# Dense products in portions of three beside a recurrence, and an earlier load of its first chunk's operands

## The chip, the cores and the metric

The kernel runs on one core of a Trainium2 chip. The metric is the time of one execution on the device, in microseconds (us). A core has a matrix engine (TensorE, in the profile PE, with its weight loads as PEld), a vector engine (VectorE, DVE), a scalar engine (ScalarE, ACT), GpSimd (POOL) and a queue engine (SyncE, SP). Each takes its own instructions strictly in order and waits on semaphores for the others; DMAs are issued from the queues of SP and ACT.

## The reference

Two residual layers over 512 positions and 1024 channels: a gated spatial MLP with its feed-forward part, then an RWKV-7 time mixer with its feed-forward part, then a last norm. The change lies in the time mixer. Cut to that:

```python
r, k, v = xr @ w_r, xk @ w_k, xv @ w_v
w = -softplus(-(w0 + tanh(xw @ w1) @ w2)) - 0.5
a = sigmoid(a0 + (xa @ a1) @ a2)
g = sigmoid(xg @ g1) @ g2
...
def step(state, inp):                       # 512 steps, 16 heads, state 64x64
    r_t, w_t, k_t, v_t, a_t, b_t = inp
    sa = einsum('bhvk,bhk->bhv', state, a_t)
    state = state * w_t + sa[..., None] * b_t + v_t[..., None] * k_t
    return state, einsum('bhvk,bhk->bhv', state, r_t)
...
y = group_norm(y) * ln_w + ln_b + bonus
return (y * g) @ w_o
```

## The kernel before

Everything is kept transposed: a tile is 128 channels by 512 positions, and there are eight of them (`KT`). A dense product is done in three matmuls of 128x512 (`mm3`, L291 to L297): the weight and the operand are each split into a high and a low part, and three of the four products are summed. The text counts such single matmuls as **dense products**; `mm3` issues three.

The recurrence is cut into eight **chunks** of 64 positions, and the sixteen heads into eight **pairs** (two heads fill 128 partitions). Within a chunk the recurrence is a small triangular system, so that the work has these stages, all in `rwkv_main`:

1. `pairs()` (L909) prepares for each pair the operands of all chunks: decays, keys, products between positions. They go to DRAM (`std`, `btd`, `vtd`) by SP's DMAs (L861, L895, L906, L790).
2. `invert(g)` (L936) inverts the 64x64 triangular blocks of four pairs: a loop of 31 steps with two DVE instructions each (L964, L965), two DVE transposes (L970, L971), copies by ACT (L975, L993, L995) and small matmuls (L985, L988).
3. `scan(g)` (L1079) walks through the eight chunks for four pairs, first `g` = 0, then `g` = 1. One chunk is a chain: L1105 and L1109 (PE, with the state) give `us` and `e`; DVE copies `us` to `wt` (L1107); L1118 applies the inverse; DVE and ACT copy the two halves to `vu` (L1119, L1120); L1125 gives the new state, which DVE adds into the next chunk's `vu` (L1128); L1130 gives the output, copied by ACT (L1133). The text calls the chunks **A0 to A7** (`scan(0)`) and **B0 to B7** (`scan(1)`). After every second chunk `finish` (L1141) normalizes the output (L1146 to L1159, with four PE transposes, L1156).
4. `load(g, c)` (L1061) brings a chunk's operands from DRAM: `st` in two DMAs of 384 KB together, `vu` in two, `cbt` in one, into rings of three tiles (`SCAN`).

Three generators hold the dense work: `projections()` (L733, the k and v products; with each v tile also `value`, L778: four matmuls L784 that count as eight instructions, one product with `wb`, L798, then DVE L800 and ACT L801), `gates()` (L998: per channel tile an operand made by ACT L1010, DVE L1011, ACT L213 and DVE L214, then six products into two accumulators) and `project()` (L1174, the output products with `w_o`).

What sets the order: `weave` (L1254) runs a main generator and after each of its yields adds `rate` portions from `fill` (a portion is what `fill` does up to its next yield) and half a step of a side generator (`invert`). A portion of `dense_steps` (L196) holds `ktiles` calls of `mm3`: with `STEPS` all 2, six products. The framework's scheduler then sets each engine's final order by its own estimates, so the written order is not the executed one. Before, `fill` holds `projections()` alone up to the end of `scan(0)`; what is left is drained, and only for `scan(1)` does `fill` become `gates()` and `project()`. `load(0, 0)` stands after the pool of the pairs is closed (L1223), in the pool that takes its place.

## Time and profile before

| | us |
|---|---|
| median of 3 runs | 1329.78 (1329.23 to 1330.55) |
| the profiled execution | 1334.18 |
| its span | 1332.4 |
| from the last dense product ahead of A0 to the end of that stretch's dense work | 752.9 to 957.8 |

A page of the profile gives busy time per engine, a view by windows gives it for stretches of time with the granted clock of PE (PEclk, 1.00 is full speed), and the timeline gives single instructions: start, duration, engine, line, operation, output and inputs, shape, count, and in brackets how long the engine had been idle and what released it. A PE duration is longer than the distance to the next start, since matmuls are pipelined; the distance between starts is what a matmul costs. A small fp32 matmul is two PE instructions.

The scans' chunks start, by their first L1105 (A0 by the end of the dense work ahead of it), at 752.9 (A0), 770.3 (A1), 779.2, 789.7, 800.3 (A4), 808.3, 816.5, 831.0 (A7), 836.1 (B0), 840.4 (B1), 858.3 (B2), 867.4, 875.1, 885.2, 900.7 (B6) and 908.8 (B7). The first instruction behind the stretch, L330, starts at 957.8.

### The profile page before, as it was taken

How to read it: one execution, taken by the hardware profiler on the slowest of the kernel's cores; microseconds unless marked ns; L12 is line 12 of the kernel's file. 1: busy time of each engine (PE TensorE's matmuls, PEld its weight loads, DVE VectorE, ACT ScalarE, POOL GpSimd, SP SyncE). 2: the span in 40 equal slices, each digit the busy share in tenths (PEclk: the TensorE clock that was granted, in tenths of full speed). 3: DMA queues.
4: the chain of work that ended last, by engine and by line, in shares of the span. 5: the costliest groups of instructions: out<-in, count | busy, mean ns of one | idle time of the engine just before them, and what ended most of it. 6: DMA issues, size and time to landing. Idle time of an engine off the chain costs nothing.

```text
span 1332.4 us, 19460 instructions
## 1 busy us (share of the span) xinstructions
PE 1277.4 (96%) x7578; PEld 1025.6 (77%) x7578; DVE 853.5 (64%) x1371; ACT 630.7 (47%) x1072; POOL 142.1 (11%) x148
## 2 busy tenths in 40 slices
PE   8999999999999999999999797799999999999996
PEld 6778888888888888677777666567888888888886
DVE  5565487887884444857788573576677777773223
ACT  5444365555553333656775443343554445452221
POOL 3100200000000001211210112123300000000001
PEclk9999999999999999999999887899999999999998
DMA  7232355555566653247778765683233333332322
GB/s 260 83 111 79 111 160 171 167 166 166 168 187 223 214 180 107 80 140 213 204 216 247 189 156 119 140 211 98 79 95 95 95 96 99 102 95 87 103 87 75
DMA packets 101100, 189.06 MB, mean 142 GB/s; under 512 B 16976, under 2 KB 48464, under 8 KB 101008
## 3 DMA queue, kind: packets, MB, share of 16 engines
q10 hardware_dynamic: 36592, 109.46, 27.1%
q1 hardware_dynamic: 64416, 78.36, 20.8%
q8 instruction: 59, 0.97, 0.3%
q14 instruction: 33, 0.27, 0.1%
HBM read 146.63 MB, written 41.16 MB: 141 GB/s over the span
## 4 chain that ended last, share of the span: by engine, by line
PE 76%; DVE 8%; DMA 4%; issue 3%; ACT 3%; POOL 1%; ACTq 0%; SPq 0%; DVEq 0%; POOLq 0%
PE mm L295 8%; PE mm L296 7%; PE mm L297 7%; PE aux L296 5%; PE aux L295 5%; PE aux L297 5%; PE us L295 5%; PE us L297 5%; PE us L296 5%; PE e L297 5%; PE e L296 5%; PE e L295 5%; DVE tt L965 1%; DVE pr L964 1%; PE e L1130 1%
## 5 line engine op out<-in xcount | busy, mean ns | idle before, releaser
L213 ACT CAST wh<-w 128x512 fp32r<-128x512 f32 x356 | 217.0, 612 | 386.4 <-PE mm L296 105.7
L214 DVE TENSOR_TENSOR wl<-w,wh 128x512 fp32r<-128x512 f32 x348 | 240.9, 693 | 180.0 <-ACT wh L213 178.6
L295 PE MATMUL mm<-mxh,wh 128*128 128x512 f32 (+1 forms) x384 | 157.4, 410 | 1.6 <-DVE h L1196 1.2
L297 PE MATMUL mm<-mxh,wl 128*128 128x512 f32 (+1 forms) x384 | 153.1, 399 | 0.4 <-DVE wl L214 0.3
L296 PE MATMUL mm<-mxl,wh 128*128 128x512 f32 (+1 forms) x384 | 152.2, 396 | 0.0
L322 POOL TENSOR_TENSOR ss<-ss,sq 128x512 f32<-128x512 f32 x30 | 41.9, 1397 | 776.5 <-issue 594.8
L518 ACT ACTIVATE cv<-z,par 128x512 f32<-128x512 f32 x88 | 71.7, 817 | 36.0 <-DVE z L516 35.9
L295 PEld LDWEIGHTS mm<-mxh,wh 128*128 128x128 f32 (+1 forms) x384 | 72.2, 188 | 20.6 <-issue 3.6
L297 PEld LDWEIGHTS mm<-mxh,wl 128*128 128x128 f32 (+1 forms) x384 | 72.3, 189 | 18.2 <-issue 0.9
L295 PE MATMUL e<-mxh,wh 128*128 128x512 f32 x216 | 84.5, 391 | 0.0
L296 PEld LDWEIGHTS mm<-mxl,wh 128*128 128x128 f32 (+1 forms) x384 | 72.6, 189 | 14.9 <-issue 0.7
L296 PE MATMUL e<-mxl,wh 128*128 128x512 f32 x216 | 84.1, 389 | 0.0
L297 PE MATMUL e<-mxh,wl 128*128 128x512 f32 x216 | 84.0, 389 | 0.0
L296 PE MATMUL aux<-mxl,wh 128*128 128x512 f32 x208 | 81.4, 391 | 2.7 <-POOL mxl L214 2.0
L295 PE MATMUL aux<-mxh,wh 128*128 128x512 f32 x208 | 81.5, 392 | 0.3 <-ACT mxh L213 0.3
L519 DVE SCALAR_TENSOR_TENSOR cv<-z,par,cv 128x512 f32<-128x512 f32 x88 | 66.1, 752 | 23.9 <-ACT cv L518 23.9
L295 PE MATMUL us<-mxh,wh 128*128 128x512 f32 x208 | 81.3, 391 | 0.0
L297 PE MATMUL aux<-mxh,wl 128*128 128x512 f32 x208 | 81.0, 389 | 0.0
L297 PE MATMUL us<-mxh,wl 128*128 128x512 f32 x208 | 81.0, 389 | 0.0
L296 PE MATMUL us<-mxl,wh 128*128 128x512 f32 x208 | 80.9, 389 | 0.0
L520 DVE SCALAR_TENSOR_TENSOR cv<-z,par,cv 128x512 f32<-128x512 f32 x88 | 66.0, 752 | 2.9
L296 PEld LDWEIGHTS aux<-mxl,wh 128*128 128x128 f32 x208 | 39.1, 188 | 12.3 <-POOL mxl L214 2.7
(1074 smaller groups left out, 2715.8 us busy)
## 6 DMA issues: line engine op xcount, KB each, us to landing
w<-in_wup ACTq DMA_DIRECT2D x88, 512.0 KB, 3.6
w<-in_wdn ACTq DMA_DIRECT2D x32, 512.0 KB, 3.6
st<-std SPq DMA_DIRECT2D x32, 384.0 KB, 5.8
std<-lq SPq DMA_DIRECT2D x32, 256.0 KB, 4.4
w<-in_wdn ACTq DMA_DIRECT2D x16, 384.0 KB, 3.2
w<-in_wsu ACTq DMA_DIRECT2D x8, 512.0 KB, 3.7
w<-in_wso ACTq DMA_DIRECT2D x8, 512.0 KB, 3.6
pw<-in_wk SPq DMA_DIRECT2D x16, 256.0 KB, 3.4
```

What stands on the lines that cost most here:

```text
L213: nc.scalar.copy(hi[r, :n], src)
L214: (lo_eng or nc.vector).tensor_tensor(lo[r, :n], src, hi[r, :n].bitcast(F32), ALU.subtract)
L295: mm(acc, wh, xh, start=first, stop=False)
L296: mm(acc, wh, xl, start=False, stop=False)
L297: mm(acc, wl, xh, start=False, stop=last)
L322: nc.gpsimd.tensor_tensor(self.ss, self.ss, self.sq, ALU.add)
L518: nc.scalar.activation(c, z[:, 2:], AF.Identity, scale=cw(2, i), bias=self.p("conv_b", l * 44 + i))
L519: nc.vector.scalar_tensor_tensor(c, z[:, 1:T + 1], cw(1, i), c, ALU.mult, ALU.add)
L520: nc.vector.scalar_tensor_tensor(c, z[:, 0:T], cw(0, i), c, ALU.mult, ALU.add)
L964: V.tensor_tensor(q, a, b, ALU.mult)
L965: V.tensor_tensor(tt[:, 0:nj, j + 1:32], tt[:, 0:nj, j + 1:32], q, ALU.add)
L1130: nc.tensor.matmul(e[H[hd], 0, i, :], pt(i, hd), vu[H[hd], hd, i, :], start=False, stop=True, skip_group_check=True)
```

## The change

Three things change. `fill` is one chain of `projections()`, `gates()` and `project()` from the start, so that the gates' products can follow the projections within `scan(0)`. In both scans a portion holds one `mm3`, and the gates yield after each of their two accumulators, while the rates go from 0.65 to 1.15 and from 0.9 to 1.6 portions per yield. And `load(0, 0)` is called ahead of the last pair's stretch: its `st` goes as eight DMAs into four free tiles of the operand ring (`mxh`, `mxl`), its `cbt` and `vu` into the scratch tiles `ss` and `rb`; the ring of three then serves A1 onwards.

```diff
-RATES = ((1.9, 2), (1.9, 6, 2.2), (0.65, 2, 1), (0.9, 2), (2, 2), (0.7, 6, 2.2))
-LEAD = 3
+RATES = ((1.9, 2), (1.9, 6, 2.2), (1.15, 2, 1), (1.6, 2), (2, 2), (0.7, 6, 2.2))
+LEAD = 4
-FIRST0, WAIT, STEPS = 1, 1, (2, 2, 2, 2, 2)
+FIRST0, WAIT, STEPS = 1, 1, (2, 2, 1, 1, 2)
...
                     self.mm3(a, self.wcols(w, k * n, n), x, k == 0, k == KT - 1)
-                yield
+                    yield
...
             ps = slice(4 * g, 4 * g + 4)
-            st = tile_([P, 4 * 3 * P + P], "st", SCAN)
-            bt, vu = tile_([P, 4, 2, C], "cbt", SCAN), tile_([P, 2, 4, C], "vu", SCAN)
-            for hd in range(2):
-                o = P * (1 - hd)
-                nc.sync.dma_start(st[H[hd], o:o + 12 * P], std[g][c, H[hd]].rearrange("p i t -> p (i t)"))
+            if g == c == 0:
+                st = [t for _ in range(2) for t in (self.xr.tile([P, T], F32, tag=tag, bufs=10, name=self.uid(tag))
+                                                    for tag in ("mxh", "mxl"))]
+                bt = scratch("ss").rearrange("p (i a f) -> p i a f", i=4, a=2)
+                vu = scratch("rb").rearrange("p (a i f) -> p a i f", a=2, i=4)
+                for i in range(4):
+                    for hd in range(2):
+                        o = P * (1 - hd)
+                        nc.sync.dma_start(st[i][H[hd], o:o + 3 * P], std[g][c, H[hd], i])
+            else:
+                t = tile_([P, 4 * 3 * P + P], "st", SCAN)
+                st = [t[:, 3 * P * i:3 * P * i + T] for i in range(4)]
+                bt, vu = tile_([P, 4, 2, C], "cbt", SCAN), tile_([P, 2, 4, C], "vu", SCAN)
+                for hd in range(2):
+                    o = P * (1 - hd)
+                    nc.sync.dma_start(t[H[hd], o:o + 12 * P], std[g][c, H[hd]].rearrange("p i t -> p (i t)"))
...
-        fill = projections()
+        fill = itertools.chain(projections(), gates(), project())
+        gw = {}
...
+        load(0, 0)
         self.weave(main, inv, fill, *RATES[5], ktiles=STEPS[1])
...
-        gw = {}
-        load(0, 0)
...
-        for _ in fill:
-            pass
-        fill = itertools.chain(gates(), project())
```

From L1064 on the changed kernel's lines stand 12 lower in the scan (L1105 becomes L1117, L1118 L1130, L1125 L1137, L1130 L1142, L1156 L1168).

**Counts by the order.** On PE the order is the same up to the first L1105. From there to L330 both kernels hold 342 dense products; by chunk:

| chunks | before | now |
|---|---|---|
| A0 | 6 | 9 |
| A1, A2, A3 | 13, 16, 7 | 12, 9, 12 |
| A4, A5, A6, A7 | 0, 0, 0, 0 | 0, 6, 6, 12 |
| B0, B1 | 0, 14 | 12, 12 |
| B2 to B6 | 18, 10, 12, 42, 14 | 12, 21, 15, 30, 15 |
| B7 and behind it | 190 | 159 |

They stand in 57 unbroken runs before and in 72 now.

**First place: PE at the start of A0.** Before (`us`, `e` are the chunk's accumulators, `st`, `vu` its loaded operands, `mm` the dense accumulator, with `wh` its weight):

```order
L297 MATMUL mm_6774<-mxh_5578,wl_6645 128x512
L1105 MATMUL us_6731<-vu_6668,st_6666 64x64
L1109 MATMUL e_6732<-vu_6668,st_6666 64x64
L1105 MATMUL us_6731<-vu_6668,st_6666 64x64 x7
L1109 MATMUL e_6732<-vu_6668,st_6666 64x64 x7
L1118 MATMUL us_6731<-wt_6741,ti_4912 64x64 x8
L784 MATMUL mm_6849<-cst,v_6772 128x128 x3
L1130 MATMUL e_6732<-vu_6668,st_6666 64x64
L784 MATMUL mm_6849<-cst,v_6772 128x128
L1125 MATMUL us_6731<-vu_6668,cbt_6667 64x64 x8
```

Now, at the same place:

```order
L1121 MATMUL e_6758<-rb_6572,mxl_6570 64x64 x2
L784 MATMUL mm_6785<-cst,v_6731 128x128 x4
L295 MATMUL mm_6733<-mxh_5585,wh_6663 128x512
L296 MATMUL mm_6733<-mxl_5586,wh_6663 128x512
L297 MATMUL mm_6733<-mxh_5585,wl_6664 128x512
L1130 MATMUL us_6757<-wt_6767,ti_4912 64x64 x8
L295 MATMUL mm_6733<-mxh_5629,wh_6663 128x512
L798 MATMUL mm_6814<-rt_4387,wb_6812 128x512
L296 MATMUL mm_6733<-mxl_5630,wh_6663 128x512
L297 MATMUL mm_6733<-mxh_5629,wl_6664 128x512
L1137 MATMUL us_6757<-rb_6572,ss_6571 64x64 x8
```

The chunk reads `rb` and the ring tiles in place of `vu` and `st`, and dense work now stands on both sides of the inverse's product (`wt`), where before nothing stood ahead of it.

**Second place: DVE between A3 and A4**, where the inverse of the second four pairs ends (`tt`, `pr`, `ix`, `li` are its tiles). Before, the start of A3's copy `wt`, now that of A4's:

```order
L800 TENSOR_TENSOR rt_4387<-mm_7090,v_6979 128x512
L970 STREAM_TRANSPOSE ix_7268<-tt_6678 128x32x32
L971 STREAM_TRANSPOSE li_7269<-tt_6678 128x32x32
L1107 COPY wt_7031<-us_7021 128x256
L1159 SCALAR_TENSOR_TENSOR rt_4386<-aux_7044,par,rt_4386 128x128 x4
L1119 COPY vu_6917<-us_7021 64x256
```

```order
L965 TENSOR_TENSOR tt_6687<-tt_6687,pr_6688 128x31
L970 STREAM_TRANSPOSE ix_7302<-tt_6687 128x32x32
L1119 COPY wt_7155<-us_7145 128x256
L800 TENSOR_TENSOR rt_4387<-mm_7212,v_7197 128x512
L971 STREAM_TRANSPOSE li_7303<-tt_6687 128x32x32
L1131 COPY vu_7047<-us_7145 64x256
```

The two transposes have moved from A3 to A4, one ahead of the copy `wt`, the other between it and the copy `vu`.

**Third place: PE in A5** (`aux` is the accumulator of four transposes and of the inverse, `mm` now that of the gates). Before, then now:

```order
L1109 MATMUL e_7235<-vu_7126,st_7124 64x64 x7
L1156 MATMUL aux_7257<-cst,y_6923 128x128 x4
L1118 MATMUL us_7234<-wt_7244,ti_4912 64x64 x8
L985 MATMUL aux_7293<-ix_7268,ti_4913 32x32 x32
L1130 MATMUL e_7235<-vu_7126,st_7124 64x64
L1125 MATMUL us_7234<-vu_7126,cbt_7125 64x64 x8
```

```order
L1121 MATMUL e_7269<-vu_7138,st_7136 64x64 x7
L1168 MATMUL aux_7291<-cst,y_6938 128x128 x4
L296 MATMUL mm_7306<-mxl_7312,w_1392_7252 128x512
L297 MATMUL mm_7306<-mxh_7311,w_1393_7253 128x512
L1130 MATMUL us_7268<-wt_7278,ti_4912 64x64 x8
L985 MATMUL aux_7333<-ix_7302,ti_4913 32x32 x32
L295 MATMUL mm_7307<-mxh_7311,wh_7254 32x512
L296 MATMUL mm_7307<-mxl_7312,wh_7254 32x512
L297 MATMUL mm_7307<-mxh_7311,wl_7255 32x512
L1142 MATMUL e_7269<-vu_7138,st_7136 64x64
L1137 MATMUL us_7268<-vu_7138,cbt_7137 64x64 x8
```

The first gate operand's products (`mxh_7311`, `mxl_7312`) have come from B1, five chunks later, and now stand ahead of the chunk's own products in PE's queue.

More of the change, by code (lines that the diff above doesn't have):

```diff
@@ L1096, in ar @@
                 def ar(i, hd, n):
-                    o = P * (3 * i + 1 + hd) + n * C
-                    return st[:, o:o + C]
+                    o = P * (1 + hd) + n * C
+                    return st[i][:, o:o + C]
                 def pt(i, hd):
-                    o = P * (3 * i + 3 * (1 - hd)) + C
-                    return st[H[hd], o:o + C]
+                    o = P * 3 * (1 - hd) + C
+                    return st[i][H[hd], o:o + C]
                 for i, hd in ih:
```

## The prediction

> **What bounds the kernel now.** The page comes first.
>
> ```profile
> span 1332.4 us, 19460 instructions
> PE 1277.4 (96%) x7578; PEld 1025.6 (77%) x7578; DVE 853.5 (64%) x1371; ACT 630.7 (47%) x1072; POOL 142.1 (11%) x148
> PEclk9999999999999999999999887899999999999998
> ```
>
> PE is the bound nearly everywhere. The one stretch in the middle where it isn't shows in the clock's row: five slices of 8 or 7 between rows of nines. The same stretch by chunks, in the view by windows:
>
> ```profile
> core 0: us, PE busy (x) PEld busy (x) DVE busy (x) ACT busy (x) POOL busy (x), PEclk, DMA share, GB/s
> 752.90:770.30 17.40, 10.09 (x95) 8.02 (x94) 13.48 (x33) 4.32 (x10) 1.30 (x2) 0.64 1.04 263
> 770.30:800.30 30.00, 28.02 (x295) 19.75 (x294) 21.02 (x48) 12.77 (x24) 5.45 (x7) 0.90 0.60 141
> 779.20:789.70 10.50, 10.18 (x107) 7.28 (x106) 8.88 (x25) 3.69 (x10) 3.27 (x4) 1.00 0.60 138
> 800.30:836.10 35.80, 28.13 (x577) 24.10 (x576) 11.96 (x29) 11.68 (x26) 8.07 (x11) 0.74 0.60 133
> 836.10:840.40 4.30, 3.48 (x82) 2.88 (x80) 2.04 (x6) 1.73 (x4) 0.81 (x1) 1.00 1.00 220
> 836.10:858.30 22.20, 16.55 (x181) 10.73 (x179) 10.53 (x21) 6.66 (x13) 3.98 (x4) 0.77 0.55 121
> 858.30:867.40 9.10, 8.85 (x99) 5.57 (x98) 6.38 (x13) 5.42 (x10) 3.36 (x4) 1.00 0.61 132
> 867.40:875.10 7.70, 7.39 (x97) 4.98 (x94) 5.12 (x13) 3.34 (x7) 1.20 (x2) 1.00 0.65 155
> 858.30:908.80 50.50, 46.92 (x514) 32.14 (x513) 38.74 (x76) 25.73 (x52) 16.11 (x16) 1.00 0.75 195
> 908.80:957.80 49.00, 47.22 (x267) 38.08 (x267) 32.55 (x53) 21.73 (x41) 16.96 (x16) 1.00 0.24 73
> 929.80:952.40 22.60, 22.22 (x97) 17.98 (x98) 15.56 (x23) 12.42 (x23) 10.20 (x11) 1.00 0.28 87
> ```
>
> By the rows A0, A1 to A3, A4 to A7 and B0 with B1, up to 858.3, PE idles 7.3 + 2.0 + 7.7 + 5.7 = 22.7 us (length less PE's busy time), and its clock is granted at 0.64, 0.90, 0.74 and 0.77: it runs at half speed for stretches. Behind 858.3 the clock is full and PE busy. Dense products are conserved (342), so the change can win idle time and clock alone, and at most what the 105.4 us up to 858.3 lose to them.
>
> **Prices.** In the row 929.8 to 952.4 stand 97 products: 22.6 / 97 = 0.233 us each. B2 takes 9.1 us with 18 of them: 9.1 - 4.2 = 4.9 us for the recurrence and four seams. B3 has 10 and four transposes: 7.7 - 2.3 = 5.4 us. A2 has 16 and a `value` step (L784, L798): 10.5 - 3.7 = 6.8 us. A warm chunk thus costs 4.9, 5.4 with transposes, 6.8 with a `value` step, plus 0.233 a dense product; B0, with none, 4.3.
>
> **A0: the early load.** The timeline, SP's row first, then PE, DVE and ACT:
>
> ```profile
> 749.23 1.15 SPq L1069 DMA_DIRECT2D st<-std  x2
> 752.51 0.39 PE L297 MATMUL mm<-mxh,wl 128*128 128x512 f32 x1
> 756.46 0.30 PE L1105 MATMUL us<-vu,st 128*64 128x64 f32 x2 [3.56 <-DMA w<-in_g]
> 761.59 0.93 PEld L1118 LDWEIGHTS us<-wt,ti 64*64 64x64 f32 x16 [3.89 <-DVE wt L1107]
> 754.92 0.37 DVE L964 TENSOR_TENSOR pr<-li,tt 128x207 f32<-128x207 f32 x1
> 761.12 0.42 DVE L1107 COPY wt<-us 128x256 f32<-128x256 f32 x1
> 757.49 0.62 ACT L213 CAST gwh<-w 128x512 fp32r<-128x512 f32 x1 [5.17 <-DMA w<-in_g]
> 758.65 0.62 ACT L226 CAST gw<-w 32x512 fp32r<-32x512 f32 x1
> ```
>
> PE waits 3.56 us at A0's first product. The view blames another DMA, but `st` was issued only at 749.2. Then 3.9 us pass for `wt`, which DVE reaches behind its inverse and gate casts. Now the operands lie ready, PE goes on at 752.9, and the order has `wt` right behind the L964 of 207 elements, which ended at 755.3: both waits go. Next is ACT: its half of `vu` now stands behind L226, which ended at 759.3, while PE, with `wt` at 755.7, will have done the inverse's product, three dense ones and L798 ahead of L1137 near 758 (an estimate at the prices above). I leave this wait of some 1.2 us within the chunk's price, which has waits of its own: A0 has 9 products and a `value` step, 6.8 + 2.1 = 8.9 us for 17.4: **-8.5**. The eight small DMAs and three others move to SP's queue in the pairs' stretch, ahead of the stores of `lq`, which DVE's L891 waits for when it reuses the buffer. Eight issues at 1.15 / 2 = 0.58 us are 4.6 us of SP.
>
> ```profile
> 730.43 12.27 SPq L895 DMA_DIRECT2D std<-lq  x4
> ```
>
> There SP spreads four issues over 12.3 us, so it has room: I take 0, bounds 0 and +2 (a store held so long that L891 waits; nothing in that stretch gets shorter). A1's loads take A0's old place at 749.2, 12 us ahead of their use.
>
> **A1 to A3.** 12, 9 and 12 products: A1 4.9 + 2.8 = 7.7, A2 6.8 + 2.1 = 8.9, A3 6.8 + 2.8 = 9.6, sum 26.2 for 30.0: **-3.8**. The half clock that stretched A1's start and A3's end goes or moves on.
>
> **A4 to A7.** Where the clock falls, and why, shows at A3:
>
> ```profile
> 789.87 1.96 DVE L970 STREAM_TRANSPOSE ix<-tt 128x1024 f32<-128x1024 f32 x1
> 791.68 1.93 DVE L971 STREAM_TRANSPOSE li<-tt 128x1024 f32<-128x1024 f32 x1
> 793.93 0.68 PE L1118 MATMUL us<-wt,ti 64*64 64x64 f32 x16 [1.66 <-DVE wt L1107]
> 793.64 3.16 ACT L975 COPY ti<-li 32x1024 f32<-32x1024 f32 x3 [2.94 <-DVE li L971]
> 835.12 1.07 PE L1130 MATMUL e<-vu,st 64*64 64x64 f32 x16 [0.93 <-DVE vu L1119]
> 795.40:805.40 10.00, 10.00 (x88) 7.65 (x88) 1.27 (x3) 5.01 (x9) 1.23 (x2) 0.50 0.00 1
> ```
>
> 1.66 us of idle behind two DVE transposes, and from 795.4 the clock, 1.00 up to 789.7, is 0.50 for 10 us. An idle time of 0.93 us at 835.1 was not followed by that (B0: 1.00). The order moves the transposes to A4, the one chunk without dense work, one of them between `wt` and `vu`, and ACT's half of `vu` behind one L975 (3.16 / 3 = 1.05 us). So A4 keeps about 4.3 us of chain and gains some 1.9 + 1.9 + 1.0 of waits and a slow clock's share: 10 us. A5 has 6 products, four transposes and the inverse's first products:
>
> ```profile
> L985 PE MATMUL aux<-ix,ti 32*32 32x32 f32 x128 | 2.4, 192 | 0.0
> ```
>
> 5.4 + 1.4 + 2.4, and 2.8 for a slow clock: 12. A6 has 6 products and the inverse's second ones, taken like the first, 4.9 + 1.4 + 2.4, and 2.3 for the clock: 11. A7 has 12: 5.4 + 2.8 = 8.2. Sum 41.2 for 35.8: **+5.4**, of which 5.6 is dense work that comes forward. The clock's terms are chosen between the ends: 31 if it stays up and nothing waits (4.9 + 5.4 + 4.9 + 5.4, 24 x 0.233 = 5.6, 4.8 for the inverse), 49 if it is as slow as before (35.8, the 24 products at twice 0.233, the transposes' 1.9); nearer to the lower, since the dense work fills three of the four chunks.
>
> **B0 and B1.** Before, PE waited for the first gate operand:
>
> ```profile
> 844.09 0.80 PE L295 MATMUL mm<-mxh,w 128*128 128x512 f32 x1 [3.24 <-ACT mxh L213]
> 876.27 0.50 PE L295 MATMUL mm<-mxh,w 128*128 128x512 f32 x1 [0.36 <-ACT mxh L213]
> 853.15 0.72 ACT L1010 ACTIVATE sq<-h,par 128x512 f32<-128x512 f32 x1
> 853.91 0.75 DVE L1011 SCALAR_TENSOR_TENSOR sq<-h,omu,sq 128x512 f32<-128x512 f32 x1 [0.45 <-ACT sq L1010]
> 854.69 0.62 ACT L213 CAST mxh<-sq 128x512 fp32r<-128x512 f32 x1 [0.82 <-DVE sq L1011]
> 852.76 0.69 DVE L214 TENSOR_TENSOR mxl<-sq,mxh 128x512 fp32r<-128x512 f32 x1 [0.36 <-ACT mxh L213]
> ```
>
> Now the operands are begun in the first scan. B0 4.9 + 2.8 = 7.7 and B1 5.4 + 2.8 = 8.2, 15.9 for 22.2: **-6.3**. Two operands per chunk cost DVE 2 x (0.75 + 0.69) = 2.9 us, ACT 2.7 us, less than a chunk of 7.7.
>
> **B2 to B6** hold 93 products for 96: **-0.7**. **B7 and behind** hold 31 fewer, at full clock: **-7.2**.
>
> Sum: -8.5 - 3.8 + 5.4 - 6.3 - 0.7 - 7.2 = -21.1 us. The runs' median, 1329.8, lies 4.4 us below the profiled execution (1334.2), and the stretch is the same in both: 1334.2 - 21.1 = 1313.1 there, 1329.8 - 21.1 = **1308.7** in the runs. More seams (72 runs for 57) have no term, since A0 to A3 have 4 or 5 runs, and B2, whose price is used, four. Their price shows here:
>
> ```profile
> 773.27 0.50 PE L295 MATMUL mm<-mxh,wh 128*128 128x512 f32 x1
> 773.60 0.40 PE L296 MATMUL mm<-mxl,wh 128*128 128x512 f32 x1
> 773.93 0.68 PE L1118 MATMUL us<-wt,ti 64*64 64x64 f32 x16
> ```
>
> Two products between small ones took 0.66 us, 0.2 over their price; if all 15 cost that on both sides, they are +6.
>
> **The rivals.**
>
> *The clock stays up* (0.12). A4's idle falls into pieces of about 2 us with products between them; if the clock needs more than such a piece, it stays up, A4 to A7 take 36 for 41.2, and A0 loses nothing: 1308.7 - 6 = 1303. Against it stands the fall behind 1.66 us at 793.9. [...]
>
> *The clock falls again* (0.20). ACT's 1.2 us in A0 lies between the 0.93 us that did nothing and the 1.66 us that did. If the clock falls there, A0 loses what it lost before, (1 - 0.64) x 17.4 = 6.3 us, and if A4 to A7 stay down to their end, 5 more: 1308.7 + 11 = 1320. For it: of the chunks' rows up to 858.3 only A2's and B0's have 1.00. [...]
>
> *Gate operands hold the recurrence* (0.06, slower). From A5 to B1 the gates' products now stand ahead of the chunk's own in PE's queue. An operand that comes late holds the chain behind it, as at 844.1. Warm, B0 and B1 would have taken 4.3 + 5.4 + 3.3 = 13.0 us; they took 22.2, 9.2 more for two operands, 4.6 each. Eight would cost 37: 1346. From 21.1 / 8 = 2.6 us each the kernel is slower. Against it: at 876.3, in the midst of the later operands, the wait was 0.36 us.
>
> *The stretch is PE's in any case* (0.04). If the matmuls' modelled ends hide that PE was full, moving work changes nothing: 1329.8. Against it are the clock's rows.
>
> **The numbers.** The forecast has 0.58. The range 1299 to 1321 takes in A4 to A7's ends (-10, +8), part of the seams and of SP (+5), the clock staying up, and its falling again. A measurement of this kernel can tell about 0.2%, 2.7 us, from no change: faster 0.58 + 0.20 + 0.12 = 0.90, same 0.04, slower 0.06.
>
> **What would show it.** A0's first product starts right behind the dense ones (no 3.56 us), and A1 near 762. PEclk 1.00 up to A4, below 1 around A4 to A6, 1.00 in B0 and B1. No wait for ACT's `mxh` over 1 us. From the last L1130 to L330 about 7 us less. It is wrong if the clock falls in A0 or B0, if A4 to A7 take over 50 us, or if the pairs' stretch ahead of 752.9 is over 2 us longer.

## The result and the profile after

The changed kernel takes 1322.18 us (median of 13 runs, 1315.05 to 1329.33), the kernel before 1332.39 beside it (13 runs, 1326.08 to 1344.60): a ratio of 0.9909, 95% interval 0.9883 to 0.9935. It is faster by about 0.9%, 10 to 12 us, for 21.1 forecast. The forecast of 1308.7 was too low by 13.5; the upper end of its range, 1321, lies 1.2 below the median. Part of this is the base: the forecast started from 1329.8 us, and beside the changed kernel the kernel before took 2.6 us more. By the ratio, the changed kernel would take 1317.7 us on the base of 1329.8.

The profiled execution took 1321.07 us. From its page:

```profile
span 1319.3 us, 19471 instructions
PE 1275.1 (97%) x7578; PEld 1023.3 (78%) x7578; DVE 852.8 (65%) x1371; ACT 631.6 (48%) x1072; POOL 140.9 (11%) x148
PEclk9999999999999999999899897999999999999998
```

PE is busy 2.3 us less than before and its span 13.1 us shorter. The clock's row has two slices below 9 from 725 us to the end of the recurrence, where before stood four (not five, as I wrote), and one earlier, near 645 us, that was not there. The view by windows: first 60 us of the pairs' stretch, then A0, A1 to A3, A4 to A7, B0 with B1, B2 to B6, B7 to L330 (columns as before: length, PE, PEld, DVE, ACT, POOL, granted clock, DMA share, GB/s).

```profile
640.00:700.00 60.00, 58.00 (x393) 43.50 (x391) 44.26 (x80) 41.32 (x78) 9.92 (x10) 0.89 0.69 190
758.10:767.20 9.10, 7.60 (x100) 5.38 (x99) 8.43 (x22) 5.16 (x12) 0.71 (x2) 1.00 1.05 247
767.20:792.10 24.90, 23.69 (x296) 16.87 (x295) 21.93 (x55) 9.14 (x21) 6.31 (x8) 1.00 0.90 214
792.10:831.70 39.60, 33.76 (x595) 25.21 (x594) 23.01 (x44) 20.54 (x36) 7.85 (x10) 0.78 0.55 128
831.70:851.40 19.70, 16.66 (x192) 10.26 (x188) 11.05 (x22) 8.14 (x16) 3.90 (x4) 0.91 0.59 147
851.40:899.50 48.10, 45.76 (x510) 33.65 (x509) 34.12 (x70) 20.60 (x43) 17.49 (x17) 0.96 0.75 205
899.50:944.70 45.20, 41.49 (x236) 33.56 (x236) 30.04 (x49) 20.05 (x37) 15.57 (x15) 0.96 0.22 68
```

The same 60 us of the kernel before:

```profile
640.00:700.00 60.00, 57.87 (x436) 43.60 (x435) 50.12 (x92) 44.01 (x84) 12.17 (x10) 1.00 0.71 199
```

Two things are to be seen. The stretch that the prediction speaks of, from the last dense product ahead of A0 to L330, takes 186.6 us for 204.9: 18 us went where 21 were forecast (with a second execution of each kernel, below, 15). But A0 begins 5 us later (758.1 for 752.9), since the clock was at half from 646.6 to 656.8 and from 670.5 to 673.9, in code that both kernels share. The two make the 13.1 us.

Three kinds of waits are new, each on a chain that the sum had as covered. In A0, ACT and then PE (a row of the timeline: start, length, engine, line, operation, operands, in brackets the idle time before it and what ended it):

```profile
756.65 0.34 ACTq L1052 DMA_DIRECT2D w<-in_g  x1
763.41 0.62 ACT L225 CAST gw<-w 32x512 fp32r<-32x512 f32 x1 [1.44 <-issue]
764.05 0.62 ACT L226 CAST gw<-w 32x512 fp32r<-32x512 f32 x1
764.70 0.37 ACT L1132 COPY rb<-us 64x256 f32<-64x256 f32 x1
765.12 0.69 PE L1137 MATMUL us<-rb,ss 128*64 128x64 f32 x16 [1.50 <-ACT rb L1132]
```

ACT's half of `vu` (`rb` in A0) stands in ACT's queue behind two casts of gate weights, which begin 6.8 us after the first of their loads is issued, and 0.06 us after the second has landed. PE waits 1.50 us for it. In A6 and B1, PE, ACT and DVE:

```profile
810.68 1.17 ACT L993 COPY tt<-aux 32x512 f32<-32x512 f32 x2
811.86 0.72 ACT L1010 ACTIVATE sq<-h,par 128x512 f32<-128x512 f32 x1
814.07 0.80 PE L295 MATMUL mm<-mxh,w 128*128 128x512 f32 x1 [2.08 <-ACT mxh L213]
841.89 0.50 PE L296 MATMUL mm<-mxl,w 128*128 128x512 f32 x1 [0.96 <-DVE mxl L214]
844.21 1.12 DVE L1171 SCALAR_TENSOR_TENSOR rt<-aux,par,rt 128x128 f32<-128x128 f32 x4 [1.91 <-PE aux L1168]
845.25 0.74 DVE L1011 SCALAR_TENSOR_TENSOR sq<-h,omu,sq 128x512 f32<-128x512 f32 x1
845.91 0.41 DVE L1131 COPY vu<-us 64x256 f32<-64x256 f32 x1
846.37 0.32 PE L1142 MATMUL e<-vu,st 64*64 64x64 f32 x2 [1.59 <-DVE vu L1131]
```

The second gate operand is begun on ACT only at 811.86, behind the inverse's copies, and PE, which has its products next in the queue, waits 2.08 us. In B1 it waits for an operand's low half, and then for DVE's half of `vu`, which stands behind an operand's L1011. Behind the last chunk, the chain of `finish`:

```profile
907.22 0.64 ACT L1158 ACTIVATE ysq<-y 128x512 f32<-128x512 f32 x1
908.05 0.68 DVE L1161 TENSOR_REDUCE gs<-ysq 128x8 f32<-128x512 f32 x1
909.01 1.64 POOL L348 TENSOR_TENSOR gr<-rs,mhalf 128x8 f32<-128x8 f32 x1 [5.26 <-DVE rs L347]
910.68 1.74 DVE L1164 TENSOR_TENSOR y<-y,gr 128x512 f32<-128x512 f32 x1 [1.75 <-POOL gr L348]
912.57 0.86 PE L1168 MATMUL aux<-cst,y 128*128 128x128 f32 x4 [2.98 <-DVE y L1164]
```

ACT, DVE, POOL and DVE hand on to each other for 5.4 us; PE has 13 dense products left to put beside it (3.0 us), where the kernel before had 42, and waits 2.98.

### The profile page after: what moved, and what is told of

Read it like the earlier page. It is cut to its first block, busy times and chain, and to the rows that moved or that the text cites. A ratio compares the mean times of both kernels' runs of the same rounds, so it can differ in the third digit from the quotient of the medians.

```text
span 1319.3 us, 19471 instructions
## 1 busy us (share of the span) xinstructions
PE 1275.1 (97%) x7578; PEld 1023.3 (78%) x7578; DVE 852.8 (65%) x1371; ACT 631.6 (48%) x1072; POOL 140.9 (11%) x148
## 5 line engine op out<-in xcount | busy, mean ns | idle before, releaser
L518 ACT ACTIVATE cv<-z,par 128x512 f32<-128x512 f32 x88 | 71.7, 817 | 35.9 <-DVE z L516 35.8
L296 PEld LDWEIGHTS aux<-mxl,wh 128*128 128x128 f32 x208 | 39.1, 188 | 12.3 <-POOL mxl L214 2.7
```

The source lines that it names most:

```text
L296: mm(acc, wh, xl, start=False, stop=False)
L518: nc.scalar.activation(c, z[:, 2:], AF.Identity, scale=cw(2, i), bias=self.p("conv_b", l * 44 + i))
```

## The experiments

Theory 1 is that the mechanism went as predicted, and that the missing part is (a) chance of the clock ahead of A0, (b) late gate operands in A6 and B1, (c) ACT's casts in A0, (d) the cover taken from the last `finish`. Theory 2 is that the change itself slows the pairs' stretch, theory 3 that the portions or the early gates are worth nothing in any case.

All lengths are read in the traces from a chunk's first product to the next chunk's, in us; "before" is the median beside which a run was made.

| kernel | median (before) | ratio, 95% interval | A0 begins | A0 | A1-A3 | A4-A7 | B0,B1 | B2-B6 | B7 to L330 | A0 to L330 |
|---|---|---|---|---|---|---|---|---|---|---|
| before | - | - | 756.5 | 13.8 | 30.0 | 35.8 | 22.2 | 50.5 | 49.0 | 201.4 |
| before again | 1333.88 (1330.66) | 1.0022, 0.9994-1.0051 | 757.5 | 13.4 | 29.0 | 32.8 | 22.0 | 50.0 | 49.0 | 196.2 |
| changed | 1322.18 (1332.39) | 0.9909, 0.9883-0.9935 | 758.1 | 9.1 | 24.9 | 39.6 | 19.7 | 48.1 | 45.2 | 186.6 |
| changed again | 1322.32 (1331.29) | 0.9921, 0.9889-0.9952 | 756.5 | 12.0 | 24.9 | 38.9 | 18.3 | 49.0 | 46.3 | 189.4 |
| early load alone | 1322.38 (1331.29) | 0.9917, 0.9889-0.9945 | 759.9 | 8.3 | 25.1 | 33.6 | 22.3 | 50.4 | 48.9 | 188.7 |
| without early load | 1327.98 (1331.29) | 0.9963, 0.9940-0.9986 | 762.5 | 9.3 | 29.9 | 37.5 | 19.6 | 47.7 | 47.0 | 190.9 |
| tail covered | 1320.06 (1331.29) | 0.9904, 0.9867-0.9941 | 752.3 | 10.3 | 25.5 | 39.4 | 21.2 | 48.4 | 43.9 | 188.8 |
| operand ahead | 1314.95 (1335.30) | 0.9863, 0.9828-0.9898 | 755.0 | 9.1 | 24.9 | 35.3 | 16.5 | 52.4 | 47.2 | 185.4 |
| casts behind | 1317.32 (1335.30) | 0.9887, 0.9852-0.9922 | 753.5 | 8.2 | 25.2 | 39.0 | 18.3 | 49.0 | 45.9 | 185.6 |
| six, chain | 1320.88 (1335.30) | 0.9910, 0.9879-0.9941 | 756.6 | 9.0 | 25.1 | 37.1 | 23.4 | 49.6 | 44.3 | 188.5 |
| three, late gates | 1322.88 (1335.30) | 0.9916, 0.9887-0.9944 | 752.6 | 9.3 | 24.9 | 34.2 | 19.8 | 51.2 | 49.3 | 188.7 |
| ahead and behind | 1315.22 (1335.37) | 0.9843, 0.9816-0.9870 | 761.0 | 8.1 | 25.2 | 34.4 | 16.5 | 47.5 | 47.0 | 178.8 |
| casts at need too | 1314.94 (1335.37) | 0.9841, 0.9808-0.9873 | 758.1 | 8.1 | 25.2 | 34.2 | 16.5 | 48.5 | 48.0 | 180.6 |
| early load, ahead | 1316.27 (1335.37) | 0.9858, 0.9827-0.9888 | 752.0 | 8.5 | 25.1 | 34.1 | 20.8 | 50.1 | 49.3 | 187.9 |

In both rows of the kernel before, A0's first product waits behind the last dense one, which ended at 752.9: from there its stretch is 204.9 and 200.8 us.

**The changed kernel again**, nothing edited.

> The changed kernel once more, nothing edited. Theory 1: the half clock at 646.6 to 656.8 and 670.5 to 673.9 us, ahead of everything that the change touches, is chance: the clock is set anew on a grid of 3.41 us, which lies differently against the program in each execution. Then this execution has its falls at other places of that unchanged code, or none: the first recurrence product starts near 753 to 755 us instead of 758.2, the falls again begin a multiple of 3.41 us apart, and the stretch from it to L330 again takes 184 to 190 us. Theory 2: the changed load order slows the pairs' stretch each time: the fall near 646 is there again and the first recurrence product starts at 757 to 759. Both: a median 9 to 14 us below the kernel before.

The pairs' stretch, A0, and A0's wait:

```profile
640.00:700.00 60.00, 58.41 (x394) 44.18 (x394) 45.03 (x81) 41.36 (x79) 8.92 (x9) 0.89 0.70 195
756.50:768.40 11.90, 8.94 (x100) 6.47 (x99) 9.35 (x23) 5.34 (x12) 1.30 (x2) 0.86 0.90 211
```

and from the timeline:

```profile
764.90 1.12 PE L1137 MATMUL us<-rb,ss 128*64 128x64 f32 x16 [2.96 <-ACT rb L1132]
```

The falls ahead of A0 came again (648.8 to 659.0, 672.6 to 676.0, and one at 546.4), which speaks for theory 2 as I had put it. The later runs, whose code is the same up to there, decide it (below). New is A0: the wait for ACT is 2.96 us and a half clock of 3.4 us stands at 764.8, so A0 takes 12.0.

**The early load alone**: the kernel before with the new `load` and `ar`, `pt`, and with

```diff
+        load(0, 0)
         self.weave(main, inv, fill, *RATES[5], ktiles=STEPS[1])
...
-        load(0, 0)
```

> The kernel before with the early load alone: the first chunk's operands loaded beside the last pair into ring tiles, old portions, rates and gates. Theory 1: A0 falls from 17.4 to about 9 us and the half clock in it goes, A1 to the end stay as before: 8 us below the kernel before (ratio 0.994), the stretch from A0 to L330 at 196 to 198 us for 204.9. Theory 2 (the early loads hold the pairs' stretch): A0 gains the same, but the first product comes 4 to 6 us later: 2 to 4 us below the kernel before.

A0, A4 to A7, B0 with B1, the tail, and B0's wait for its first gate operand:

```profile
759.90:768.30 8.40, 7.29 (x100) 5.57 (x99) 7.12 (x21) 3.27 (x8) 0.02 (x1) 1.00 1.05 253
793.40:827.00 33.60, 27.14 (x581) 23.45 (x580) 17.77 (x41) 16.11 (x30) 8.10 (x11) 0.75 0.63 143
827.00:849.30 22.30, 16.65 (x180) 10.79 (x179) 10.52 (x21) 6.66 (x13) 3.98 (x4) 0.77 0.52 119
899.70:948.60 48.90, 47.11 (x268) 38.05 (x267) 32.53 (x53) 21.71 (x41) 16.99 (x16) 1.00 0.23 72
```

and from the timeline:

```profile
834.95 0.80 PE L295 MATMUL mm<-mxh,w 128*128 128x512 f32 x1 [3.23 <-ACT mxh L213]
```

A0 to A3 take 33.4 us at full clock, for 47.4 from the last dense product on in the kernel before; the rest stays as it was, its wait of 3.2 us in B0 too. The run is as fast as the whole change (0.9917 for 0.9921). I had expected 8 us here and the other half of the gain from the rest of the change; the early load brought 9 to 11, and beside it the rest brings nothing that the runs can tell.

**Without the early load**: the changed kernel with `load(0, 0)` back behind `ctx.close()`, into tiles of the pool.

```diff
-            if g == c == 0:
+            if False:
...
-        load(0, 0)
         self.weave(main, inv, fill, *RATES[5], ktiles=STEPS[1])
...
+        load(0, 0)
         next(inv)
```

> The changed kernel without its early load: the first chunk's operands are loaded where the kernel before loads them; portions of three, rates and the chain of gates stay. Theory 1 (the parts add): A0 takes 15 to 18 us again, with its wait of 3 to 4 us at the first product and a half clock; the rest keeps the 10 us that it gained in the profiled executions: 3 to 6 us below the kernel before in the medians, 184.5 + 8.4 = about 195 us from A0 to L330. Rival (the portions alone bring nothing, the gain is the early load's): within 2 us of the kernel before.

The time is inside the expectation (0.9963), and the stretch, 190.9 us, is shorter than the 195 of it, but A0's wait isn't where I had it. The order now puts eight transposes and six dense products ahead of A0's first product (762.5), which doesn't wait, and the wait is for `wt`:

```profile
766.23 0.68 PE L1130 MATMUL us<-wt,ti 64*64 64x64 f32 x16 [1.82 <-DVE wt L1119]
```

The clock falls once there (766.9 to 770.3). With 0.9917 and 0.9963 the two parts don't add to 0.992: beside the early load, the 5 us of the portions are gone. I read it so that what they had won was cover for the late load.

**The tail covered**, 12 more products held back from the second scan:

```diff
-RATES = ((1.9, 2), (1.9, 6, 2.2), (1.15, 2, 1), (1.6, 2), (2, 2), (0.7, 6, 2.2))
+RATES = ((1.9, 2), (1.9, 6, 2.2), (1.15, 2, 1), (1.45, 2), (2, 2), (0.7, 6, 2.2))
```

> The changed kernel with the rate of the second scan at 1.45 instead of 1.6 portions a step: 25 dense products instead of 13 lie between the last recurrence product and the last chunk's transposes (L1168). Theory 1: the 2.98 us wait at the last L1168 was a cover that the change took away; 12 products x 0.233 = 2.8 us more of it bring the wait under 0.7 us, the half clock behind it (912.8 to 916.2) goes, and the stretch from B7 to L330 loses those 3 us plus 1 to 2 of clock: 3 to 4 us below the changed kernel. Rival: the 12 products are missed in the chunks B2 to B7, where waits of the recurrence open: 0 to 1 us below it, or above.

B7 to L330, and the first wait left there:

```profile
897.10:941.10 44.00, 42.70 (x247) 34.53 (x246) 30.39 (x52) 20.56 (x39) 15.62 (x15) 1.00 0.22 68
```

and from the timeline:

```profile
911.58 0.39 PE L295 MATMUL aux<-sg,gwh 128*128 128x256 f32 x1 [0.93 <-DVE rt L1171]
```

The wait at L1168 is gone and the clock stays at 1.00: PE idles 1.3 us there instead of 3.7. This tail holds 9 products more than the changed kernel's (168 for 159 from B7 on), 2.1 us, and is still 1.3 to 2.4 us shorter, so the missing cover cost 3.4 to 4.5 us. But the products are missed ahead of it: in B2 to B6 PE idles 6.2 us instead of 2.3 and 3.9, and B0 with B1 take 21.2 us for 19.7 and 18.3, at a clock of 0.77. The runs show 0.9904 beside 0.9921: the rival's 0 to 1 us can't be excluded. The wait is moved rather than removed.

**Gate operands one portion ahead**:

```diff
-            for k in range(KT):
-                with ExitStack() as behind:
+            def ready(k):
+                with ExitStack() as behind:
...
-                    x = self.operand(t)
+                    return self.operand(t)
+
+            x = ready(0)
+            for k in range(KT):
+                ahead = ready(k + 1) if k + 1 < KT else None
                 for a, w, n in zip(accs, ws, (P, 32)):
                     self.mm3(a, self.wcols(w, k * n, n), x, k == 0, k == KT - 1)
                     yield
+                x = ahead
```

> The changed kernel with each gate operand begun one portion ahead: ACT and DVE make operand k + 1 before PE is given the products of operand k. Theory 1 (late operands cost what A4 to B1 gain too little): the waits of 2.07 to 2.09 us in A6 and of 0.97 and 1.59 us in B1, and the half clocks of 7 to 14 us behind the first, shrink to waits under 0.7 us; A4 to B1, 57.2 to 60.6 us in three executions, take 51 to 55, and the kernel is 3 to 6 us below the changed one. Rival (the waits are the recurrence's own, of queues on ACT and DVE that stay as full): A4 to B1 take 57 to 61 again, within 1.5 us of the changed kernel.

A4 to A7, B0 with B1, B2 to B6, and the rows of a new wait in B3 (here L1137 is ACT's half of `vu` and L1142 the product behind it):

```profile
789.00:824.30 35.30, 30.54 (x601) 22.52 (x600) 23.47 (x46) 21.67 (x38) 7.86 (x10) 0.90 0.63 143
824.30:840.90 16.60, 15.76 (x196) 10.39 (x192) 12.09 (x26) 9.55 (x19) 3.83 (x4) 1.00 0.70 166
840.90:893.30 52.40, 45.36 (x503) 33.59 (x502) 31.86 (x65) 17.94 (x39) 17.15 (x16) 0.90 0.75 191
```

and from the timeline:

```profile
861.66 1.14 ACT L213 CAST wh<-w 128x512 fp32r<-128x512 f32 x2 [12.35 <-DMA w<-in_wo]
863.25 1.12 PE L1142 MATMUL us<-vu,cbt 128*64 128x64 f32 x16 [2.98 <-ACT vu L1137]
```

A4 to B1 take 51.9 us, for 59.3 and 57.2 of the changed kernel: the waits of 2.08, 0.96 and 1.59 us are gone, B0 and B1 are at full clock, and A4 to A7 are at half for 6.8 us instead of 17.1 and 13.7. Theory 1 holds for this stretch. It gives back 3 to 4 us in B2 to B6, where ACT waits 12.35 us for the first output weight, with its half of `vu` queued behind the casts: A0's wait at another place. The runs give the edit 6 to 8 us (0.9863 for 0.9909 and 0.9921), the stretch in the traces 1 to 4 (185.4 for 186.6 and 189.4); where the rest of it lies isn't shown.

**ACT's casts behind its half of `vu`**:

```diff
+                if g == c == 0:
+                    r.first_vu = self.last(mybir.EngineType.Activation)
...
-            self.stack(ws, w32[0:32, 512:], False)
+            with ExitStack() as behind:
+                if g == 0:
+                    behind.enter_context(tc.issue_after(r.first_vu))
+                self.stack(ws, w32[0:32, 512:], False)
```

> The changed kernel with ACT's casts of the gate weights queued behind its half of the first chunk's vu, which in the changed kernel stands behind two of them and so behind the landing of the weights. Theory 1: the wait at A0's L1137, 1.50, 1.90 and 2.96 us in three executions, falls below 0.6, and the half clock of 3.4 us that followed it in two of the three is not there: A0 takes 7.3 to 8 us instead of 9.1 to 12.0, and the kernel is 2 to 4 us below the changed one. Rival (another wait is just behind, of DVE's half or of A1's): A0 and A1 together stay at 16 to 18 us, within 1 us of the changed kernel.

A0, and its wait (L1142 is the former L1137):

```profile
753.50:761.60 8.10, 7.53 (x100) 5.34 (x99) 7.63 (x22) 3.94 (x9) 0.51 (x1) 1.00 1.06 260
```

and from the timeline:

```profile
759.50 0.69 PE L1142 MATMUL us<-rb,ss 128*64 128x64 f32 x16 [0.57 <-ACT rb L1135]
```

0.57 us for 1.50, 1.90 (tail covered) and 2.96, no fall of the clock, and A0 in 8.2, just over the 7.3 to 8 expected. With A1 to A3 0.3 longer, the gain in the stretch is 1 to 4 us, as theory 1 had it. The runs, 0.9887 beside 0.9909 and 0.9921 with intervals of about 0.3%, agree with that but don't show it.

**Portions of six with the chain of gates**, and **portions of three with late gates**, the early load in both:

```diff
-RATES = (..., (1.15, 2, 1), (1.6, 2), ...)
-LEAD = 4
-FIRST0, WAIT, STEPS = 1, 1, (2, 2, 1, 1, 2)
+RATES = (..., (0.65, 2, 1), (0.9, 2), ...)
+LEAD = 3
+FIRST0, WAIT, STEPS = 1, 1, (2, 2, 2, 2, 2)
...
-                    yield
+                yield
```

> The early load and the one chain of dense work kept, but portions of six products and the rates and the lead of the kernel before. Theory 1 (bringing the gates forward only moves time from B0 to the end into A4 to A7, whatever the portions): A4 to A7 take 38 to 42 us, B0 and B1 18 to 21, the tail 44 to 47, and the time is within 3 us of the changed kernel and of the early load alone, about 1322. Theory 2 (even small portions are what gains): waits of the recurrence stand behind six products and the chunks A0 to A3 or B2 to B6 are 3 or more us longer: 1326 or more.

```diff
-        fill = itertools.chain(projections(), gates(), project())
+        fill = projections()
...
+        for _ in fill:
+            pass
+        fill = itertools.chain(gates(), project())
         self.weave(scan(1, left.pop()), None, fill, *RATES[3], ktiles=STEPS[3])
```

> The early load, portions of three and the new rates kept, but the gates begin only with the second scan, as in the kernel before. Theory 1 (neither the portions nor the early gates bring more than 3 us): A4 to A7 33 to 36 us, B0 with B1 22 to 25 with a wait of about 3 us for the first gate operand, time 1320 to 1326, like the early load alone. Theory 2 (small portions cost seams of 0.2 us each): 3 to 6 us above the early load alone, spread over A0 to A3 and B2 to B6.

0.9910 and 0.9916. With the early load alone (0.9917) and the whole change (0.9921) these make a square of neither, one, the other and both, all alike, and their stretches are alike too: 188.7, 188.5, 188.7, and 186.6 or 189.4. In the first, A4 to A7 took 0.9 less than expected (37.1), B0 and B1 2.4 more (23.4). In the second, B0's wait for the first operand came back smaller, 1.35 us for 3.2, and B0 with B1 took 19.8, under the 22 to 25 expected. Neither costs seams that can be seen: theory 3, as long as the operands come late.

**Ahead and behind**: the edits of `ready` and of `first_vu` together.

> The changed kernel with the gate operands one portion ahead and ACT's casts of the gate weights behind its half of the first chunk's vu, both. Theory 1 (late operands and the casts are two separate losses): A0 7.5 to 8.5 us, A4 to B1 51 to 55, B2 to B6 about 52 as with the operands ahead alone, and a time 2 to 4 us below that kernel: 1311 to 1314. Rival (the two gains were the same luck of the clock's windows): 1315 to 1318.

A4 to A7, B0 with B1, B2 to B6, and the wait left at the last transposes (L1178 is the former L1168):

```profile
794.40:828.70 34.30, 30.49 (x601) 22.18 (x600) 22.89 (x44) 21.64 (x38) 7.87 (x10) 0.90 0.64 148
828.70:845.30 16.60, 15.77 (x196) 10.41 (x192) 12.08 (x26) 9.54 (x19) 3.83 (x4) 1.00 0.71 171
845.30:892.80 47.50, 42.95 (x502) 31.89 (x501) 32.05 (x65) 17.97 (x39) 16.95 (x16) 0.96 0.78 210
```

and from the timeline:

```profile
906.41 1.08 PE L1178 MATMUL aux<-cst,y 128*128 128x128 f32 x4 [3.02 <-DVE y L1174]
```

The stretch is 178.8 us, 7.8 and 10.6 below the changed kernel's, and every stage but the last is below its forecast or at most 0.6 above. The median, 1315.22, lies in the rival's 1315 to 1318 and not in theory 1's 1311 to 1314, and doesn't show a gain against the kernel with the operands ahead (1314.95); the ratios, 0.9843 and 0.9863, each with an interval of 0.3%, don't part them. Of the two profiled executions this one began A0 at 761.0, the other at 755.0, which hides 6 us of their difference. So the two losses are separate in the trace, at two places, and in time the second edit's gain isn't shown. The gain in B2 to B6 (47.5 for 52.4) wasn't expected: a wait there was shorter, as the next run explains.

**Output weights cast at need**, added to that: the loads stay early, `cast()` is called half a product tile before its use.

```diff
-                        w = ws.take()
+                        w = nxt or cast()
+                        nxt = None
...
+                        if n == 1 and m % 2 == 1 and m < KT - 1:
+                            nxt = cast()
```

> As the run with both, and the casts of each output-projection weight (behind B2) are queued on ACT half a product tile before their use instead of as soon as their load is issued. Theory 1 (ACT's half of vu standing behind a cast that waits for a weight's load is one mechanism, at A0 and at B2 to B4): the waits of 1.77 us for the first weight and 2.98 us for vu in the kernel with the operands ahead fall below 1 us each, or the second does; B2 to B6, 52.4 us there, take 46 to 49, and the time is 2 to 4 us below the run with both. Rival (the products themselves then wait for the casts at need): within 1 us of it or above.

ACT's half of `vu` in B3:

```profile
861.75 0.37 ACT L1140 COPY vu<-us 64x256 f32<-64x256 f32 x1 [10.78 <-DVE vu L1139]
```

No cast stands ahead of it now, and PE doesn't wait for it. In the run with both that wait had shrunk to 0.73 us, though in the same place of the queue, since the weight's load landed 6.3 us after its issue there and 8.4 in the kernel with the operands ahead. So the mechanism is the same as in A0, and there was little left to take: PE waits 1.77 us for a weight as before, the clock is at half for 6.8 us instead of 3.4, B2 to B6 take 48.5 for 47.5, and the time is the same. In time the rival holds.

**The early load with operands ahead**, portions of six and late gates as in the kernel before: the early load alone with the edit of `ready`.

> The early load alone, with the gate operands one portion ahead, but portions of six, old rates, and the gates beginning in the second scan as before. Theory 1 (portions of three and early gates do gain, but late operands ate it): B0 and B1 fall by 2 to 4 us from 22.3, the time is 1318 to 1321, and the run with both stays 5 us or more below it. Theory 2 (portions and early gates are worth nothing in any case): 1311 to 1316, like the run with both.

1316.27, at the edge of theory 2 and 1.05 us above the run with both, where theory 1 wanted 5; B0 and B1 fell by 1.5 us (20.8), less than theory 1's 2 to 4. The run that differs by the portions and the early gates alone is the one with the operands ahead: its stretch is 2.5 us shorter (185.4 for 187.9), and its ratio no better (0.9863 for 0.9858). With the casts behind as well, the stretch is 9.1 us shorter (178.8), and the runs show 2 (0.9843 for 0.9858, each with 0.3%, 4 us). Which it is stays open. So does another thing: against the early load alone the runs give the operands ahead 8 us (0.9858 for 0.9917), and the two traces 0.8 (187.9 for 188.7).

**The kernel before again**, nothing edited.

> The kernel before, nothing edited, for a second profile. Theory 1 (the clock's falls ahead of the recurrence depend only on where the 3.41 us grid lies against the program, in either kernel): if the grid lies otherwise than in its first profile, it too has falls at 544 to 546, 618 to 620 or 646 to 650 us, and its last dense product ahead of the recurrence ends at 756 to 762 instead of 752.9; the stretch from there to L330 stays at 198 to 206 us, against 184 to 190 of the changed kernel. Theory 2 (those falls belong to the changed kernel's order): none of them, and 752 to 753 again. If the grid lies as in its first profile, the two give the same.

The pairs' stretch, and A0 from the last dense product on:

```profile
640.00:700.00 60.00, 58.10 (x431) 43.71 (x430) 48.98 (x90) 43.36 (x82) 11.83 (x10) 0.97 0.71 194
752.85:770.90 18.05, 10.78 (x96) 8.66 (x95) 13.33 (x32) 4.36 (x10) 1.30 (x2) 0.63 0.96 231
```

One fall, 665.2 to 668.6, where no other execution has one, and the same end at 752.85. The grid lay nearly as in the first profile, so by itself this profile doesn't part theories 1 and 2. The granted clocks of the runs add something: over 69 runs of the kernel before they go from 0.968 to 0.982, 86 down to 48 us at half clock (an estimate, twice the missing share of the span, as the two kernels' first profiles have grants of 1.00 and 0.50 alone), and the two profiled executions have 0.975 and 0.977. So this kernel too has executions with some 20 us more of half clock than its profiles show, though not where.

**Where the clock falls ahead of A0.** In the fourteen executions of the table, which share the code up to some 670 us, every fall begins a whole number of 3.4133 us from every other of its execution: the clock is set on a grid. I took the first L814 product, at 584 to 586 us in all, as a mark in the program and measured how far it lies behind the grid's last edge:

| mark behind the edge, us | executions | half clock begins, ahead of 700 us |
|---|---|---|
| 0.17, 0.66, 0.80, 0.91, 0.91 | early load with ahead; before again; before; three late gates; tail covered | none; one at 665.2; none; none; none |
| 1.69 to 2.74 | changed again; operand ahead; without early load; six, chain; changed; casts at need | 646.5 to 648.8 in all six, 544 to 546 in five, 670 to 673 in all six |
| 2.83, 3.01, 3.23 | early load alone; ahead and behind; casts behind | 618 to 619 in all three, 650 in the first two, 669.6 to 673.8 in all three |

The falls at 646 to 650 and 670 to 674 follow the place on the grid, and kernels with identical code there (tail covered, changed again) stand in different rows. The rows' bounds were drawn after the fact, and the falls at 544 to 546 lie ahead of the mark and move it: the changed kernel and casts at need, 0.01 us apart at the mark, differ in that fall. Another fall, at 726 to 735, is in all fourteen, 10.24 us long, but 3.41 in changed again, operand ahead and casts behind. The recurrence can begin between 752.0 and 752.9 in the executions of the first row, and at 753.5 to 761.0 in the others (without early load at 762.5, behind the products named above). Tail covered has the changed kernel's code up to the second scan, and its clock stays up:

```profile
640.00:700.00 60.00, 57.90 (x439) 43.40 (x437) 50.15 (x94) 44.23 (x85) 12.21 (x10) 1.00 0.76 212
```

Theory 2 falls, since three executions with the early load began A0 at 752.0 to 752.6; (a) is shown. The same wait in the two profiled kernels, before and changed:

```profile
645.57 0.49 PE L814 MATMUL e<-lr,l 128*128 128x512 f32 x1 [0.99 <-ACT l L729]
```

```profile
645.10 0.50 PE L814 MATMUL e<-lr,l 128*128 128x512 f32 x1 [0.95 <-ACT l L729]
```

Before, an edge lies at 645.1 and cuts the 0.99 us in two halves, and PE is busy 85% and 86% of the two windows (a window is the time between two edges); in the changed kernel the 0.95 us lie whole between the edges at 643.2 and 646.6, PE is busy 72% of that window, and at its end the clock falls.

## Why the prediction was right or wrong, point by point

The terms against the means of the two executions of each kernel:

| term | predicted | measured | with ahead and behind |
|---|---|---|---|
| A0 (with the wait ahead of it) | -8.5 | 10.5 for 17.7: -7.2 | -9.6 |
| A1 to A3 | -3.8 | 24.9 for 29.5: -4.6 | -4.3 |
| A4 to A7 | +5.4 | 39.3 for 34.3: +5.0 | +0.1 |
| B0, B1 | -6.3 | 19.0 for 22.1: -3.1 | -5.6 |
| B2 to B6 | -0.7 | 48.6 for 50.3: -1.7 | -2.8 |
| B7 to L330 | -7.2 | 45.8 for 49.0: -3.2 | -2.0 |
| sum | -21.1 | -14.8 | -24.2 |

**A0: right in kind, 1.3 short.** The 3.56 and 3.9 us of waits went, as forecast, and the early load alone gives all of the gain that the runs can tell (0.9917 for 0.9921). The step that failed is ACT's wait of "some 1.2 us within the chunk's price". I took the end of L226 from the old trace, 759.3; but the cast waits for a load, and its time was not the same: PE waited 1.50, 1.90 and 2.96 us in three executions of this code, in the last two with 3.4 us of half clock. That was the rival "the clock falls again", which holds for A0 in those two.

**A1 to A3: right**, by the clock staying at 1.00.

**A4 to A7: right as a sum, in part by luck.** The clock fell where forecast (800.2 and 813.8). Of its two causes, A4's transposes and the second gate operand, only the first stands in the sum. A4 and A5 together took 18.2 and 18.9 us in the two executions for 22 forecast, and A6, with the late operand, 13.5 and 12.3 for 11; the two errors offset each other. Operands in time take 4 to 5 us off.

**B0 and B1: wrong by half.** The step was "Two operands per chunk cost DVE 2 x (0.75 + 0.69) = 2.9 us, ACT 2.7 us, less than a chunk of 7.7." That compares sums of busy time; but PE has a gate product in its queue ahead of the recurrence's own, and what counts is when ACT and DVE begin that one operand, behind copies and L1171. It is the rival "gate operands hold the recurrence" at a small price: three waits (one in A6, two in B1) of 4.6 us together and the half clocks behind them, where it asked for 4.6 each. With operands ahead the stage takes 16.5 for 15.9 forecast.

**B2 to B6: right.**

**B7 and behind: wrong by 4.0.** The 31 products left as counted (190 and then 159 from B7 on). The step "at full clock: -7.2" took them all as bare time. Some were the cover of the last `finish` chain: PE's idle time there rose from 1.8 to 3.7 us and 3.4 to 6.8 us were at half clock. The prediction didn't ask what these products had hidden.

**SP and the pairs' stretch: 0 was right**, as the three executions with the early load show that began A0 at 752.0 to 752.6. The sign of being wrong, "the pairs' stretch ahead of 752.9 is over 2 us longer", came true (5.2 us), for a reason outside the change: my test didn't have the clock's chance in it. The stated stretch is 186.6 to 189.4 for 200.8 to 204.9.

**The base of the sum.** That "the stretch is the same in both", the profiled execution and the runs, was wrong: the sum stood on one execution of 1334.2 us with a stretch of 204.9, and the second one, at 1329.97 close to the median of 1329.8, has 200.8. So some 2 us of the forecast (4 us, if the second execution is the typical one) were that execution's own.

**From the stages to the runs.** Against the 14.8 us of the stages' means stand 10 to 12 us in the runs. The granted clocks of the runs narrow this down: their means are 0.9745 over 69 runs of the kernel before and 0.9792 over 19 of the changed one, which are 68 and 55 us at half clock, 13 us less, or 6.5 us of time (estimates from these clocks and the spans). In the profiled executions the stretch from A0 to L330 lost 18.8 us of half clock (means of 44.4 and 25.6), or 9.4 us of time. So 3 us of what is missing in the runs is time at half clock. Whether it fell ahead of A0 or behind it stays open.

**The signs.** A0's first product came right behind the dense ones, and A1 9.1 us later in the first execution, as forecast. The clock in B0 and B1 was 0.91 and not 1.00, the wait for `mxh` 2.08 us and not under 1, and in the second execution the clock fell in A0.

**Seams** as a loss: not seen. **The clock stays up**: not the case (27.3 us at half between A0 and L330, 47.8 before). **The stretch is PE's in any case**: excluded by the early load's gain.

The operands of the first chunk are the gain. The portions of three and the early gates brought 0.9963 without the early load, and beside it nothing that the runs can tell. The whole with operands ahead and casts behind beats both kernels, 0.9843 (0.9816 to 0.9870) of the kernel before, for 0.9909 (0.9883 to 0.9935).

## What to carry to other kernels

Work that is moved away was cover for something: before counting it as gained, look for the chain that ran beside it, at the place it leaves (here `finish`, with a wait of 2.98 us at L1168). An operand made on engines with queues of their own is in time or late by what stands ahead of it in each queue, not by the sum of their busy times (B0 and B1 took 19.0 us for the 15.9 of the sums, and 16.5 with the operands begun earlier); begin it one portion before its use, and never queue a link of a recurrence behind a cast that waits for a load (PE waited 1.50 to 2.96 us in A0, and 0.57 with the casts behind). And compare two single profiles only from a mark behind their shared code: kernels with the same code up to some 670 us began A0 up to 9 us apart.

## What the runs showed of the hardware

- The clock is set on a grid of 3.4133 us that doesn't start with the program's stages: all half-clock intervals inside the 14 executions (but for the last, cut off by the end) are whole multiples (3.41, 6.83, 10.24, 13.65, 17.1, 20.5 us), and the mark in the program lies 0.17 to 3.23 us behind an edge. In the first profile of each kernel every change of the clock fits this grid within 1 ns. In the changed kernel's it fell behind a single 0.95 us of idle in a window of which PE was busy 72%, and with PE busy 100% of each window it stayed at half for three (646.6 to 656.8 us).
- PE's busy share of a window alone doesn't tell whether the clock falls behind it. In the changed kernel's first profile the windows from 728.5, 844.6 and 858.2 us, with 52%, 53% and 66%, were followed by a fall, those from 762.6 and 793.4, with 56% and 59%, not (nor the one from 750.9 in the kernel before, with 58%), and the one from 667.1 with 88%, nearly all small products of 64 rows or two columns, by one. What else sets it isn't shown.
- The same two loads of a gate weight let the first cast begin 6.8 us after the first was issued in one execution of the changed kernel and 8.2 us in another; a copy queued behind it took that difference over as PE's wait (1.50 and 2.96 us).
